# Moving tiles within 128 bytes: start addresses of tails, convolution, gate and keys in a two-layer decoder trunk

## The chip, the cores and the metric

One of the cores of a Trainium2 chip runs the whole program. The metric is device time in microseconds of that core. The times shown are three runs of the kernel before; the profile is of one further execution of the same program.

## What is computed

The reference is a trunk of two layers, on one sequence of 512 tokens with 1024 channels in float32. Each layer is a half-step SwiGLU feed-forward block (FFN), a token mixer and another half-step FFN. The mixer of the first layer is a short gated convolution, that of the second is native sparse attention (NSA). Each sub-layer normalises its input and modulates it with a shift, a scale and a gate computed from a conditioning vector:

```python
h = adaln(x, norm_g[i, 0], shift[:, 0], scl[:, 0])
x = x + HALF * gate[:, 0, None, :] * swiglu(h, ffn_w_in[i, 0], ffn_w_out[i, 0])
h = adaln(x, norm_g[i, 1], shift[:, 1], scl[:, 1])
y = short_conv_mixer(h, ...) if i % N_MIXERS == 0 else nsa_mixer(h, ...)
x = x + gate[:, 1, None, :] * y
h = adaln(x, norm_g[i, 2], shift[:, 2], scl[:, 2])
x = x + HALF * gate[:, 2, None, :] * swiglu(h, ffn_w_in[i, 1], ffn_w_out[i, 1])
```

`swiglu` is `(silu(g) * u) @ w_out` with `g, u = h @ w_in` and 2816 hidden channels. There are four FFNs, one convolution and one NSA.

## The kernel before, in words

The kernel keeps x as eight tiles of 128 channels by 512 tokens. Weights are streamed from HBM as 128x1024 tiles. Every product is made of three matmuls (`mm3`, lines 179 to 181): operand and weight are split into a high and a low part of type float32r (`split`, line 170 on ScalarE, line 171 on VectorE), and high x high, high x low and low x high are summed. In a matmul the weight tile is the held operand (it is loaded into the array by an LDWEIGHTS), and the activation is the streamed one, with 512 columns (all tokens) or 256 (one half of them). The names in the profile are, for example, `gu<-hhi,whi`: output, streamed, held.

The stages follow each other in program order: FFN 0 (`ffn_first`), convolution (`conv`), FFN 1 and 2 (`ffn`), NSA (`nsa`), FFN 3 (`ffn`).

- `ffn_first` and `conv` begin with a head start (`hs`) on a few weight tiles while the normalised input h is still being made, and go on with 512-column products: `gu` in `ffn_first`, `cv` in `conv`. In the FFNs `Hidden` holds the activated hidden channels as tiles `ahi` and `alo` in the pool `fa`; the output products `y` stream them.
- `ffn` makes its head start with 256 columns, then a gate (one weight tile `wh`, `wl`, on the two halves of h), one more pair, and then `seven_products` for the other 18 hidden blocks j = 4 to 21. These multiply by blocks of 2x2 with seven products instead of eight; they stream h and the tiles `th`, `tl` made by `Norm.quarters` and hold `whi`, `wlo`, `qah`, `qal`, `qbh` and `qbl`. After blocks of hidden channels come output products `y`, three rounds of 144 matmuls in each `ffn`.
- Each FFN and the mixers end with a tail (`ty`): the last output products, done for the first 256 tokens and then for the others, so that the norm of the next stage (sums of squares on line 264, reciprocal root on lines 210 to 218, spread over the partitions by the matmul on line 272, then `Norm.piece` on lines 321 to 324) can begin on the first half. In `ffn` the tail has four weight tiles; the last two are split into the buffers of `th`, `tl` (tags t..2 and t..0).
- In `conv` the tail's three weight tiles are in a pool of their own, `tw`. In NSA, keys `K` are streamed against held queries `Q` (line 1068, `s<-k,q`).

The order on each engine is that of the program, but for parts marked as of high priority. A tile waits for the last readers of the buffer that it takes over. All DMAs of weights are issued by SyncE, but for an accumulating one by GpSimd on line 516.

Where a tile begins in a partition is settled by the allocator. Pools are stacked from both ends of SBUF, those with `side="right"` from the top down. `shift(p, n)` (a tile of n bytes that nothing reads or writes) moves what is stacked after it. As the listing stands before the change, the starts within 128 bytes are: 0 for `fa` (`ahi`, `alo`), for the weight pools `wp` and `ada`, for `sw` (`qah`, `qal`, `qbh`, `qbl`), for h in `ffn_first` and `conv`, for z in `conv`, and for K and Q; 64 for h in `ffn` and `nsa`, for `th` and `tl` (and so for the gate's `wh`, `wl`, which use the same buffers) and for `tw`.

Of the kernel before, what the change touches and what calls it, by code (L numbers as in the profile page):

```python
# [13 lines left out]
F32 = mybir.dt.float32  # L14
F32R = mybir.dt.float32r
# [7 lines left out]
P = 128  # L23
D = 1024
T = 512
HT = T // 2
KD = D // P
# [26 lines left out]
def decoder_kernel(ctx, tc, xT, cT, ng, adaw, adab, ffi, ffo, cwi, cw, cwo,  # L54
# [3 lines left out]
    def pool(es, name, bufs, **kw):  # L58
        kw.setdefault("reuse_waits", "tile")
        return es.enter_context(tc.tile_pool(name=name, bufs=bufs, **kw))  # L60


    def shift(p, n):
        p.tile([P, n // 4], F32, name="shift")
# [118 lines left out]
    def weights(src, nk, ncol, own=None, held=3, raws=None, to=None, added=False):  # L183
        def part(name, dt, bufs, from_):
            return (from_ or wp).tile([P, nk * ncol], dt, name=name, tag=name, padded_shape=[P, KD * P], bufs=bufs)

        hi, lo = to or (part("whi", F32R, held, own), part("wlo", F32R, held, own))
        raws = raws or own
        raw = part("wraw", F32, 3 if raws in (None, wp) else 2, raws)
        nc.sync.dma_start(raw.rearrange("p (a n) -> p a n", a=src.shape[1]), src)  # L190
        if added:
            split_added(raw, src, hi, lo)
        else:
            split(raw, hi, lo)
        return [t.rearrange("p (k n) -> p k n", n=ncol) for t in (hi, lo)]
# [28 lines left out]
    class Halves:  # L224
        def __init__(self, *t):
            self.t = t
# [5 lines left out]
    class Norm:  # L232
# [91 lines left out]
            nc.vector.scalar_tensor_tensor(self.lo[d][:, a:b], xr, sh, hi, op0=ALU.add, op1=ALU.subtract)  # L324

        def quarters(self, tt):
            self.th, self.tl = [[tt.tile([P, KD // 2, HT], F32R, name=f"t{e}{j}", tag=f"t{e}{j}") for j in range(4)] for e in "hl"]
            for d in range(KD):
                nc.scalar.activation(self.full[:, d], self.full[:, d], AF.Identity, bias=mod(self.s, 1, d))
            n = KD // 2  # L330
            b11, b12 = self.full[:, 0:n, 0:HT], self.full[:, 0:n, HT:T]
            b21, b22 = self.full[:, n:KD, 0:HT], self.full[:, n:KD, HT:T]
            t = b11, b22, b12, b21
            nc.vector.tensor_tensor(t[0], b11, b12, ALU.subtract)
            nc.vector.tensor_tensor(t[2], b22, b12, ALU.subtract)
            nc.vector.scalar_tensor_tensor(t[1], t[0], -1.0, b22, op0=ALU.mult, op1=ALU.subtract)
            nc.vector.scalar_tensor_tensor(t[3], t[1], -1.0, b21, op0=ALU.mult, op1=ALU.subtract)
            for j in (2, 0, 3, 1):
                split(t[j], self.th[j], self.tl[j])
            self.blocks = [(lambda i, j=j: (self.th[j][:, i, :], self.tl[j][:, i, :])) for j in range(4)]  # L340
# [62 lines left out]

    class Hidden:
        def __init__(self, es, bufs):
            self.fa = pool(es, "fa", bufs, side="right")
            self.hi, self.lo = [], []

# [83 lines left out]
    def ffn(s, f, nrm, nxt, w0, ahead):  # L492
        with ExitStack() as es:
            hp = pool(es, "hp", 1)
            hid = Hidden(es, 12)
            keep = hid.keep
            nj = 2
# [58 lines left out]
                keep(e[:, 0:2].rearrange("p a b -> p (a b)"))  # L556

            js = [(j, c) for j in range(nj) for c in range(2)]
            shift(pool(es, "gap", 1, side="right"), 448)
            tt = pool(es, "tt", 1, side="right")  # L560
            swa = pool(es, "swa", 1, side="right")
            with ExitStack() as tf_es:
                nrm.alloc_seven(hp, pool(tf_es, "tf", 1))
                h = nrm.hi, nrm.lo
                with ExitStack() as hw_es:
                    hw = pool(hw_es, "hw", 1)
                    shift(hw, 64)
                    w = w0 + [weights(ffi[f, j, c], KD, P, hw, 1, wp) for j, c in js[len(w0):]]

                    gate = weights(ffi[f, nj, 0], KD, P, to=[tt.tile([P, D], F32R, name="w" + e, tag=f"t{e}1") for e in "hl"])  # L570
                    os = head_start(nrm, h, [(lambda k, w=w_: (w, 0, k)) for w_ in w])
                os += pair(f, nj, h, gate=gate)
                nrm.quarters(tt)
            sw_es = es.enter_context(ExitStack())

            own, quarter = (partial(swa.tile, [P, 2, KD * P // 2], F32, name="qa", bufs=2),
                            [partial(hp.tile, [P, 2, KD * P // 2], F32, name="qa", tag=t) for t in ("hhi1", "hlo1")])
            sums = chain((own, own, own), cycle((*quarter, own, own)))
            sw = pool(sw_es, "sw", 1)
            shift(sw, 64)  # L580
            for j in range(nj + 1):
                hid.activate(os[2 * j], os[2 * j + 1])
# [2 lines left out]
            for p, (j0, j1) in enumerate(FOUR):  # L585
# [3 lines left out]
                a = (hid.hi[j0:j1], hid.lo[j0:j1])  # L589
                if p < len(FOUR) - 1:  # L590
                    outputs(range(KD), lambda d: ffn_out(f, d, 1, j0, j1), a, n,
                            lambda d, o: nc.vector.scalar_tensor_tensor(x[d], o, mod(s, 2, d), x[d], op0=ALU.mult, op1=ALU.add))  # L592
            sw_es.close()


            ws = []
            for i, d in enumerate(range(0, KD, 2)):
                if i < 2:
                    ws.append(ffn_out(f, d, 2, j0, j1))
                else:  # L600
                    t = (2, 0)[i - 2]
                    to = [tt.tile([P, KD // 2, HT], F32R, name=f"t{e}{t}").rearrange("p a b -> p (a b)") for e in "hl"]
                    raw = swa.tile([P, 2, KD * P // 2], F32, name="qa", bufs=2).rearrange("p a b -> p (a b)")
                    nc.sync.dma_start(raw.rearrange("p (a n) -> p a n", a=2),
                                      ffo[f, d:d + 2, :, j0 * P:j1 * P].rearrange("d p c -> p d c"))
                    split(raw, *to)
                    ws.append([t.rearrange("p (k n) -> p k n", n=P) for t in to])
# [22 lines left out]
    def conv(s, nrm, nxt, extra, w0, ahead, own):  # L630
        with ExitStack() as es:
            h_es = es.enter_context(ExitStack())
            hp = pool(h_es, "hp", 1)
            shift(hp, 256)
            ca = pool(es, "cva", 2, side="right")
            h = nrm.alloc(hp)
            ks = [(k, k) for k in range(KD)]
            zh, zl = [], []
            fill = spread(extra, 2 * KD - 3)
            for d in range(KD):  # L640
                if d == 0:
                    w = w0 + [weights(cwi[3], KD, P, own)]
                    *os, nx = head_start(nrm, h, [(lambda k, w=w_: (w, 0, k)) for w_ in w])
                else:
                    os = [nx] if d == 1 else []
                    for c in range(len(os), 3):
                        w = weights(cwi[3 * d + c], KD, P, own if (d + c) % 2 else None)
                        o = psum("cv")
                        project(o, w, 0, h, ks, True, True)
                        os.append(o)  # L650
                cg, v, b = os
                cs = tmp("cs")
                nc.scalar.activation(cs, cg, AF.Copy)
                u = ca.tile([P, T + 2], F32, name="u")
                nc.vector.memset(u[:, 0:2], 0.0)
                nc.vector.tensor_mul(u[:, 2:], cs, v)
                y = tmp("yc")
                nc.vector.tensor_scalar(y, u[:, 2:], cws[:, 2 * KD + d:2 * KD + d + 1], None, op0=ALU.mult)
                for i in (1, 0):
                    nc.vector.scalar_tensor_tensor(y, u[:, i:i + T], cws[:, i * KD + d:i * KD + d + 1], y,  # L660
                                                   op0=ALU.mult, op1=ALU.add)
                z = tmp("z")
                nc.vector.tensor_mul(z, y, b)
                hi = ca.tile([P, T], F32R, name="zhi", bufs=KD)
                lo = ca.tile([P, T], F32R, name="zlo", bufs=KD)
                split(z, hi, lo)
                zh.append(hi)
                zl.append(lo)
                fill()
            z = (zh, zl)  # L670
            h_es.close()
            tw = pool(es, "tw", 1, side="right")
            for d in range(KD - 3):
                w = weights(cwo[d], KD, P)
                o = psum("y")
                project(o, w, 0, z, ks, True, True)
                residual(s, d, o, nxt)
                fill()
            assert not extra
            return tail(s, nxt, [(d, weights(cwo[d], KD, P, tw), 0, ks) for d in range(KD - 3, KD)], z, ahead)  # L680
# [26 lines left out]
    def nsa(s, nrm, nxt, w0, ahead):  # L707
        with ExitStack() as es:
            na = pool(es, "na", 1, side="right")
# [99 lines left out]
            def run(jobs):  # L809
                for j in jobs:  # L810
                    j()

            K = [[na.tile([P, T], F32R, name=f"k{b}{e}") for e in range(2)] for b in range(2)]
            Q = [na.tile([P, T], F32R, name=f"q{q}") for q in range(NG)]
            keys, heads = turners(qn, kn, K, Q)
            with ExitStack() as hw_es:
# [529 lines left out]
```

## Time and profile before

| what | value |
|---|---|
| time, median of 3 runs | 1957.31 us (1955.87 to 1958.6) |
| profiled execution | 1955.17 us, span 1953.4 us |
| TensorE busy, matmuls | 1902.4 us (97%), 12600 |
| VectorE / ScalarE / GpSimd busy | 1456.4 (75%) / 883.6 (45%) / 211.6 us (11%) |
| granted TensorE clock | 1.0 over the span |
| HBM read | 308.15 MB, 159 GB/s over the span |

The page's first part gives the busy time of each engine; a busy TensorE need not be at its peak, because matmuls overlap in the pipeline. A group's row gives its line, engine and operation, the names out<-in, the shape, the count, the busy time, the mean of one in ns and the idle time before it. A matmul's duration includes its way through the pipeline; how fast matmuls follow each other is read from their start times in the timeline.

### The profile page before, as it was taken

Reading aid. Unit: us, or ns where it says so; the run is one execution under the profiler, and the core shown is the slowest. Engines: PE = TensorE matmul, PEld = TensorE weight load, DVE = VectorE, ACT = ScalarE, POOL = GpSimd, SP = SyncE. Lnnn points to the kernel's source line nnn. Section 1 sums busy time; section 2 is a strip of 40 time slices with the busy share of each in tenths; the row PEclk is TensorE's granted clock in tenths of the full one; section 3 lists DMA queues with packets and bytes.
Section 4 is the critical chain, followed back from the end, with each engine's and each line's share of the span. In section 5 each row is a group of like instructions: output and inputs, shape, how many; then the busy total and the mean of one; then the engine's idle time right before and its main releaser. Section 6 shows DMA issues by size and latency. Waiting matters only on the chain.

```text
span 1953.4 us, 32342 instructions
## 1 busy us (share of the span) xinstructions
PE 1902.4 (97%) x12600; PEld 1725.7 (88%) x12600; DVE 1456.4 (75%) x2557; ACT 883.6 (45%) x1425; POOL 211.6 (11%) x302
## 2 busy tenths in 40 slices
PE   5999999999999999999999999999999899999999
PEld 3878888898899898999989899999888789898989
DVE  7878888674467596878859687885787878686965
ACT  3322222242236353444635343465888966353532
POOL 0000000100010000000000000001445630000000
PEclk9999999999999999999999999999999999999999
DMA  8888899522235564634556453235423523765621
GB/s 311 303 321 325 313 320 328 205 98 97 67 120 162 155 173 132 160 103 126 156 156 173 134 158 103 78 130 139 112 60 68 125 74 113 188 167 143 173 82 65
DMA packets 113671, 313.42 MB, mean 160 GB/s; under 512 B 13996, under 2 KB 14268, under 8 KB 113517
## 3 DMA queue, kind: packets, MB, share of 16 engines
q1 hardware_dynamic: 96300, 274.02, 41.2%
q0 software_dynamic: 17216, 37.33, 11.1%
q8 instruction: 99, 1.62, 0.3%
q14 instruction: 56, 0.45, 0.1%
HBM read 308.15 MB, written 3.15 MB: 159 GB/s over the span
## 4 chain that ended last, share of the span: by engine, by line
PE 85%; DVE 7%; ACT 4%; issue 2%; DMA 1%; SPq 0%; POOL 0%; DVEq 0%; ACTq 0%
PE gu L181 13%; PE gu L180 13%; PE gu L179 13%; PE y L179 7%; PE y L180 7%; PE y L181 7%; PE hs L180 2%; PE hs L179 2%; PE hs L181 2%; PE cv L179 2%; PE cv L181 2%; PE cv L180 2%; PE ty L180 2%; PE ty L179 1%; PE ty L181 1%
## 5 line engine op out<-in xcount | busy, mean ns | idle before, releaser
L170 ACT ACTIVATE whi<-wraw 128x1024 fp32r<-128x1024 f32 (+2 forms) x274 | 270.7, 996 | 507.3 <-PE y L180 218.3
L171 DVE TENSOR_TENSOR wlo<-wraw,whi 128x1024 fp32r<-128x1024 f32 (+2 forms) x274 | 312.9, 1147 | 57.9 <-ACT whi L170 55.6
L179 PE MATMUL gu<-hhi,whi 128*128 128x256 f32 (+1 forms) x880 | 277.6, 315 | 0.0
L181 PE MATMUL gu<-hhi,wlo 128*128 128x256 f32 (+1 forms) x880 | 277.5, 315 | 0.0
L180 PE MATMUL gu<-hlo,whi 128*128 128x256 f32 (+1 forms) x880 | 277.5, 315 | 0.0
L179 PE MATMUL y<-ahi,whi 128*128 128x512 f32 x587 | 228.6, 389 | 0.0
L180 PE MATMUL y<-alo,whi 128*128 128x512 f32 x587 | 228.5, 389 | 0.0
L181 PE MATMUL y<-ahi,wlo 128*128 128x512 f32 x587 | 228.3, 389 | 0.0
L125 DVE CUSTOM_DVE_ANT_0 adaraw<-adaraw,cond 128x1024 f32<-128x1024 f32 x144 | 174.8, 1223 | 40.4 <-DMA adaraw<-in_adaw 38.2
L180 PEld LDWEIGHTS gu<-hlo,whi 128*128 128x128 f32 x880 | 165.1, 188 | 12.2
L179 PEld LDWEIGHTS gu<-hhi,whi 128*128 128x128 f32 x880 | 165.2, 188 | 12.1
L181 PEld LDWEIGHTS gu<-hhi,wlo 128*128 128x128 f32 x880 | 165.2, 188 | 12.0
L516 POOL DMA_DIRECT2D qa<-in_ffi x54 | 65.0, 1205 | 793.2 <-DMA qa<-in_ffi 275.9
L179 PEld LDWEIGHTS y<-ahi,whi 128*128 128x128 f32 x587 | 110.2, 188 | 23.3 <-issue 0.8
L181 PEld LDWEIGHTS y<-ahi,wlo 128*128 128x128 f32 x587 | 110.2, 188 | 23.1
L180 PEld LDWEIGHTS y<-alo,whi 128*128 128x128 f32 x587 | 110.2, 188 | 22.5
L592 DVE SCALAR_TENSOR_TENSOR x<-y,mods,x 128x512 f32<-128x512 f32 x72 | 53.4, 750 | 92.5 <-PE y L181 92.4
L179 PE MATMUL gu<-th,qbh 128*128 128x256 f32 x432 | 119.5, 277 | 1.0 <-ACT qbh L170 1.0
L181 PE MATMUL gu<-th,qbl 128*128 128x256 f32 x432 | 119.6, 277 | 0.6 <-DVE qbl L171 0.5
L180 PE MATMUL gu<-tl,qbh 128*128 128x256 f32 x432 | 119.3, 276 | 0.0
L179 PE MATMUL gu<-th,qah 128*128 128x256 f32 x432 | 119.2, 276 | 0.0
L180 PE MATMUL gu<-tl,qah 128*128 128x256 f32 x432 | 119.2, 276 | 0.0
(312 smaller groups left out, 5094.8 us busy)
## 6 DMA issues: line engine op xcount, KB each, us to landing
adaraw<-in_adaw SPq DMA_DIRECT2D x144, 512.0 KB, 6.0
wraw<-in_ffi SPq DMA_DIRECT2D x122, 512.0 KB, 4.0
qa<-in_ffi SPq DMA_DIRECT2D x108, 256.0 KB, 3.7
qa<-in_ffi POOLq DMA_DIRECT2D x54, 512.0 KB, 6.3
wraw<-in_ffo SPq DMA_DIRECT2D x72, 384.0 KB, 3.9
a<-in_ffi SPq DMA_DIRECT2D x54, 256.0 KB, 4.5
wraw<-in_cwi SPq DMA_DIRECT2D x24, 512.0 KB, 3.3
wraw<-in_nwi SPq DMA_DIRECT2D x20, 512.0 KB, 3.8
```

The costliest lines, as they stand in the source:

```text
L125: nc.vector.tensor_tensor_reduce(out=raw, in0=raw, in1=cond, scale=1.0, scalar=0.0, op0=ALU.mult, op1=ALU.add, accum_out=m)
L170: nc.scalar.activation(hi, src, AF.Copy)
L171: nc.vector.tensor_tensor(lo, src, hi, ALU.subtract)
L179: nc.tensor.matmul(o, sh, mh, start=first, stop=False)
L180: nc.tensor.matmul(o, sh, ml, start=False, stop=False)
L181: nc.tensor.matmul(o, sl, mh, start=False, stop=last)
L516: nc.gpsimd.dma_start(qa, bass.AP(tensor=a21.tensor, offset=a21.offset, ap=[a21.ap[0], [0, 2], a21.ap[1]]), accum_op=ALU.add)
L592: lambda d, o: nc.vector.scalar_tensor_tensor(x[d], o, mod(s, 2, d), x[d], op0=ALU.mult, op1=ALU.add))
```

## The change

No instruction is added or taken away. Seven places move tiles:

- `Hidden` stacks 64 bytes before `fa`, so `ahi` and `alo` begin 64 bytes within 128 (in all four FFNs); in `ffn` the later shift of 448 becomes 384, so `th` and `tl` stay at 64.
- The buffers of tags th1 and tl1 are 128 bytes longer; the gate uses them from byte 64 on, so `wh` and `wl` begin at 0.
- The last two weight tiles of the tail in `ffn` go to the buffers of `qah` and `qal` in the pool `sw` (0) instead of `th2`, `tl2`, `th0`, `tl0` (64); `sw` is closed with the other pools.
- `conv`: h moves by 64 (256 becomes 320), and 64 bytes are stacked before the pool of z, so z begins at 64 and `tw`, stacked after it, at 0.
- `nsa`: 64 bytes before K and 64 after, so K begins at 64 and Q, stacked after it, stays at 0.

```diff
         def quarters(self, tt):
-            self.th, self.tl = [[tt.tile([P, KD // 2, HT], F32R, name=f"t{e}{j}", tag=f"t{e}{j}") for j in range(4)] for e in "hl"]
+            self.th, self.tl = [[tt.tile([P, T * KD // 4 + 32 * (j == 1)], F32R, name=f"t{e}{j}", tag=f"t{e}{j}")[:, 0:T * KD // 4]
+                                 .rearrange("p (a b) -> p a b", b=HT) for j in range(4)] for e in "hl"]
...
         def __init__(self, es, bufs):
+            shift(pool(es, "fs", 1, side="right"), 64)
             self.fa = pool(es, "fa", bufs, side="right")
...
-            shift(pool(es, "gap", 1, side="right"), 448)
+            shift(pool(es, "gap", 1, side="right"), 384)
...
-                    gate = weights(ffi[f, nj, 0], KD, P, to=[tt.tile([P, D], F32R, name="w" + e, tag=f"t{e}1") for e in "hl"])
+                    gate = weights(ffi[f, nj, 0], KD, P, to=[tt.tile([P, D + 32], F32R, name="w" + e, tag=f"t{e}1")[:, 16:16 + D] for e in "hl"])
...
-            sw_es = es.enter_context(ExitStack())
-
...
-            sw = pool(sw_es, "sw", 1)
+            sw = pool(es, "sw", 1)
...
-            sw_es.close()
...
-                    t = (2, 0)[i - 2]
-                    to = [tt.tile([P, KD // 2, HT], F32R, name=f"t{e}{t}").rearrange("p a b -> p (a b)") for e in "hl"]
+                    to = [sw.tile([P, 2, KD * P // 2], F32R, name=f"qa{e}", bufs=2).rearrange("p a b -> p (a b)") for e in "hl"]
...
-            shift(hp, 256)
+            shift(hp, 320)
+            shift(pool(es, "cs", 1, side="right"), 64)
             ca = pool(es, "cva", 2, side="right")
...
+            na.tile([P, 16], F32, name="shift")
             K = [[na.tile([P, T], F32R, name=f"k{b}{e}") for e in range(2)] for b in range(2)]
+            na.tile([P, 16], F32, name="shift2")
             Q = [na.tile([P, T], F32R, name=f"q{q}") for q in range(NG)]
```

## The prediction

> **What bounds the kernel now.** I read the page's totals and its chain of waits first.
>
> ```profile
> span 1953.4 us, 32342 instructions
> PE 1902.4 (97%) x12600; PEld 1725.7 (88%) x12600; DVE 1456.4 (75%) x2557; ACT 883.6 (45%) x1425; POOL 211.6 (11%) x302
> PE 85%; DVE 7%; ACT 4%; issue 2%; DMA 1%; SPq 0%; POOL 0%; DVEq 0%; ACTq 0%
> ```
>
> TensorE sets the end: 85% of the chain, and no other engine has more than 7%. A nanosecond per matmul is worth 12.6 us, so the question is at what step the matmuls follow each other, and what depends on the addresses there. I write 64/0 for "streamed operand begins 64, held operand 0 bytes within 128"; these starts are sums of tile sizes in the listing, not readings of the profile. The next view is the groups of matmuls by form (busy time, then mean ns of one).
>
> ```profile
> L179 PE MATMUL y<-ahi,whi 128*128 128x512 f32 x587 | 228.6, 389 | 0.0
> L179 PE MATMUL gu<-th,qah 128*128 128x256 f32 x432 | 119.2, 276 | 0.0
> L179 PE MATMUL cv<-hhi,whi 128*128 128x512 f32 x160 | 62.3, 389 | 0.0
> L180 PE MATMUL y<-zlo,whi 128*128 128x512 f32 x40 | 15.6, 389 | 0.0
> L180 PE MATMUL ty<-alo,whi 128*128 128x256 f32 x138 | 39.3, 285 | 0.0
> L180 PE MATMUL ty<-alo,th 128*128 128x256 f32 x96 | 27.0, 281 | 0.0
> L180 PE MATMUL ty<-zlo,whi 128*128 128x256 f32 x48 | 13.5, 281 | 0.0
> L180 PE MATMUL gu<-hlo,wh 128*128 128x256 f32 x48 | 13.6, 283 | 0.0
> ```
>
> The form is the same 128x256 in five of these rows, but one takes 276 ns (64/0: the seven products), one 283 (64/64: the gate), one 285 with its waits (0/0: the tails) and two 281 (0/64: tails with th or z). A duration holds the pipeline too; the step comes from starts in the timeline (column 1 is the start).
>
> ```profile
> 610.73 0.28 PE L180 MATMUL gu<-hlo,whi 128*128 128x256 f32 x1
> ...
> 620.59 0.28 PE L180 MATMUL gu<-hlo,whi 128*128 128x256 f32 x1
> ...
> 1937.85 0.28 PE L179 MATMUL ty<-ahi,whi 128*128 128x256 f32 x1
> ...
> 1943.49 0.28 PE L181 MATMUL ty<-ahi,wlo 128*128 128x256 f32 x1
> 1943.61 0.28 PE L179 MATMUL ty<-ahi,th 128*128 128x256 f32 x1
> ...
> 1949.15 0.28 PE L181 MATMUL ty<-ahi,tl 128*128 128x256 f32 x1
> ```
>
> At 64/0, 87 steps take 9.86 us, 0.1133 each. At 0/0, 47 steps take 5.64 us, 0.1200. At 0/64, 47 steps take 5.54 us, 0.1179. So duration less about 163 ns is the step, and a 256-column matmul could lose 6.7 ns (from 0/0 or 64/64) or 4.5 ns (from 0/64). A 512-column one at 0/0 already goes at 389 - 163 = 226, twice 113: it has nothing to win.
>
> **The change part by part.** No instruction is added or removed; tiles move.
>
> *256-column matmuls brought to 64/0.* Rows have three lines each (L179, L180, L181), so counts are three times a row's. Tails on whi/wlo: 3 x 138 = 414, from 0/0, 414 x 6.7 ns = 2.8 us. Tails on the FFN's last weights: 3 x 96 = 288, from 0/64, 1.3 us. Tail of the convolution: 3 x 48 = 144, from 0/64, 0.65 us. Gate: 144, from 64/64, 0.96 us. Head start of the convolution, whose h moves from 0 to 64:
>
> ```profile
> L179 PE MATMUL hs<-hhi,whi 128*128 128x256 f32 x34 | 9.6, 283 | 0.0
> L179 PE MATMUL hs<-hhi,whi 128*128 128x256 f32 x36 | 9.9, 276 | 0.0
> ```
>
> The first row is that head start (409 to 421 us), the second the same code in an FFN (929 to 941 us), already at 64/0. It has 4 jobs x 8 x 2 halves x 3 = 192, 1.3 us. Together 7.0 us.
>
> *What of it reaches the end.* The last tail (1926 to 1949 us) has nothing behind it but the output: 0.64 + 0.43 = 1.1 us in full. The gate lies ahead of a wait in the same stage, so I looked at what that wait hangs on (chain of waits, start, length, what):
>
> ```profile
> 620.52 0.13 PE gu L181
> 620.65 0.23 SPq L513
> 620.97 0.39 SPq L513
> 621.42 6.11 DMA a<-in_ffi
> 627.55 0.64 ACT qbh L170
> ```
>
> The transfer that ACT waits for is issued when a TensorE group behind the gate ends, so it moves with TensorE and the gate's gain passes. It is otherwise in the tails before a norm. There the second half runs beside VectorE's reciprocal root, residuals and weight splits (windows; busy and count of PE, PEld, DVE, ACT):
>
> ```profile
> 390.70:397.30 6.60, 6.60 (x53) 6.42 (x53) 6.04 (x21) 2.73 (x4) 0.00 (x0) 1.00 0.25 82
> 907.00:917.20 10.20, 10.20 (x84) 9.95 (x84) 9.06 (x28) 5.17 (x10) 0.00 (x0) 1.00 0.30 104
> ...
> 917.25 0.28 PE L181 MATMUL ty<-ahi,tl 128*128 128x256 f32 x1
> 918.29 0.75 PE L179 MATMUL hs<-hhi,whi 128*128 128x256 f32 x4 [0.76 <-ACT hhi L323]
> ```
>
> VectorE is busy 92% and 89% there, and TensorE then stands until ACT has hhi: a faster second half only lengthens that wait. I count the second half of those three tails as covered: FFN 2 x (48 x 6.7 + 48 x 4.5) = 1.1 us, first tail 63 x 6.7 = 0.4 us. If the cover is thinner than it looks, up to 1.5 us more comes through. Sum: 7.0 - 1.5 = 5.5 us.
>
> *The tail's last weights in sw instead of tt.* Their first buffer is then free after the product with s1 of j = 20, not of the last j; the second is freed by the same product of j = 21 as before. Nothing is later, so 0.
>
> *Keys at 64.* The profile has no 64/0 row of this form among the scores; 64 matmuls of 128x256 stand between 0 and 64 x 6.7 = 0.4 us. Their stage is full of waits on VectorE, so I take 0.
>
> *512-column matmuls that also go from 0/0 to 64/0.* These come along because hid, h and z move: y on ahi/alo 3 x 587 = 1761, cv 480, y on z 120, in all 2361. The only 64/0 run of 512 columns in the trace is the NSA gates' projection:
>
> ```profile
> L179 PE MATMUL gl<-hhi,whi x8: 390/394/394, 1330.8 to 1335.6; 128*128 128x512 f32 x8
> L180 PE MATMUL gl<-hlo,whi x8: 388/388/398, 1331.0 to 1335.8; 128*128 128x512 f32 x8
> L181 PE MATMUL gl<-hhi,wlo x8: 392/392/394, 1331.3 to 1336.1; 128*128 128x512 f32 x8
> ```
>
> Medians 394, 388, 392 make 391.3 on average, 2.3 ns above the 389 of 0/0, and it stays so over all 24. At that price: 2361 x 2.3 ns = 5.4 us, as much as is won. But the step is not a function of the residues alone. The same line with the same operands has two steady values:
>
> ```profile
> L179 PE MATMUL hs<-hhi,whi 128*128 128x256 f32 x14 | 3.9, 279 | 0.0
> L180 PE MATMUL nat<-wlo,hhi 128*128 128x256 f32 x27 | 7.6, 281 | 0.0
> L180 PE MATMUL nat<-wlo,hhi 128*128 128x256 f32 x31 | 8.6, 276 | 0.0
> ```
>
> hs at 64/0 ran at 279 to 280 from 1261.8 to 1266.5 us and at 276 in the FFN row above; nat at 0/64 ran at 281 (1285 to 1294 us) and at 276 (1350 to 1361 us). A run keeps the step it entered with until something disturbs it. gl was entered from such a slower stretch; the y blocks will be entered from gu at 276. Bounds 0 and +5.4 us; I take 0, because the state ahead of y is the fast one in all seven-product rows. A gain below 226 per step has no row and is left out.
>
> Against the profiled execution (1955.17 us: span 1953.4 plus 1.8) this gives 1949.7; the median shown, 1957.31, lies 2.1 above that execution, so 1957.3 - 5.5 = **1951.8 us**.
>
> **The rivals.**
>
> *The wide matmuls take the slower step.* For it: gl, 24 of 24. Against it: gl's entry. With all 2361, -5.5 + 5.4, 1957.2 us; with one group alone (first FFN's y 465: +1.1; conv 600: +1.4; other y 1296: +3.0) 1952.9 to 1954.8.
>
> *The tails stay in the slow state.* The sums of squares interrupt each tail, and each re-entry may land at 281. Then 0/0 and 64/64 win 750 x 2.2 ns = 1.6 us and the rest nothing; with the cover about 1.3: 1956.0 us. Against it: of the FFN head starts that such interruptions cut up, most run at 276.
>
> *Slower: the y blocks hand a slow step on.* Now y at 0/0 always hands over to gu at 276. If y at 64/0 hands it 281, the seven products behind it (16 per FFN x 84 x 3 FFNs = 4032) each lose 4.5 ns: 18.1 us, with y's own 3.0: 1951.8 + 21.1 = 1972.9 us. The place is the first gu after each y block; it decides from 5.5 + 3.9 = 9.4 us of loss, about 2100 of those matmuls. For it: the hs row at 279, which is 64/0. Against it: the other 64/0 rows.
>
> *The addresses do nothing.* The steps would belong to the stages, not to the starts, and nothing changes: 1957.3 us. Against it: one code line, one form, 283 and 276 in two head starts. The Trainium skill ("TensorE: Matmul & The Clock Gate", "Step-by-step: what each phase is for") says that streamed operand and weights have independent read ports, so that "Loading the next tile's weights doesn't steal SBUF read bandwidth from the running matmul", and ("SBUF — State Buffer", "Who interferes with whom") that PE never waits on anyone. By that rule this rival is right; the trace disagrees, with 283 against 276.
>
> **How the numbers follow.** Forecast 0.49; wide matmuls slower 0.25; tails slow 0.10; slow step handed on 0.10; nothing 0.06. About 0.2%, 3.9 us, is what a measurement here tells from no change. Faster than 1953.4: nearly all of the forecast and a little of the second case, 0.48. Slower than 1961.2: the fourth and a little more, 0.11. The rest, 0.41, is the same. The likeliest case alone reaches from 1949.9 (7.0 + 0.4, no cover) to 1953.5 (one tail or one group slow). The range for 8 in 10 takes in the wide matmuls' 1957.2 and no change with its scatter: 1949.9 to 1958.0.
>
> **What would show it.** In the groups by form: ty at 276 to 278 instead of 281 to 285, gu<-hlo,wh 276, the conv head start 276: these show the gain. y and cv at 389 show the wide ones unharmed, 391 the second case. gu<-th at 276 clears the fourth, 280 confirms it. The wait before hs at 918 longer by about 0.5 us shows the cover. The prediction is wrong if the 256-column rows keep their durations, or if they fall and the span does not.

## The result

The change made the kernel slower: 1978.32 us (median of 4 runs, 1975.47 to 1979.94) against 1957.95 us before (4 runs, 1955.87 to 1958.84). The ratio is 1.0103, 95% interval 1.0088 to 1.0118, which is +20.4 us. The prediction was 1951.8 us.

The page of the kernel after: totals and the chain of waits by engine.

```profile
span 1976.3 us, 32341 instructions
PE 1922.0 (97%) x12600; PEld 1731.4 (88%) x12600; DVE 1457.1 (74%) x2557; ACT 885.6 (45%) x1425; POOL 211.7 (11%) x302
PE 85%; DVE 7%; ACT 4%; DMA 2%; issue 2%; SPq 0%; POOL 0%; DVEq 0%; ACTq 0%
```

TensorE still sets the end with the same 12600 matmuls, and its busy time rose by 19.6 us, most of the 22.9 us by which the span grew. The busy times of the other engines changed by 2 us or less. So the matmuls became slower, and the groups by form (busy time, then mean ns of one) say which:

```profile
L179 PE MATMUL y<-ahi,whi 128*128 128x512 f32 x587 | 232.7, 396 | 0.0
L179 PE MATMUL gu<-th,qbh 128*128 128x256 f32 x432 | 120.6, 279 | 1.7 <-ACT qbh L170 1.7
L180 PE MATMUL cv<-hlo,whi 128*128 128x512 f32 x160 | 62.7, 392 | 0.0
L180 PE MATMUL ty<-alo,whi 128*128 128x256 f32 x138 | 38.6, 279 | 0.0
L180 PE MATMUL ty<-alo,qah 128*128 128x256 f32 x96 | 26.6, 277 | 0.0
L180 PE MATMUL y<-zlo,whi 128*128 128x512 f32 x40 | 15.8, 395 | 0.0
L180 PE MATMUL ty<-zlo,whi 128*128 128x256 f32 x48 | 13.5, 280 | 0.0
L180 PE MATMUL gu<-hlo,wh 128*128 128x256 f32 x48 | 13.2, 276 | 0.0
```

The small rows behaved as hoped: the tails fell from 285 and 281 ns to 279 and 277, the gate from 283 to 276. The wide rows paid for it: y on hidden went from 389 to 396, y on z from 389 to 395, cv from 389 to 392. And gu on th, whose operands mostly stayed where they were, rose from 276 or 277 to 277 with qah and 279 with qbh. The timeline of one output block and what follows it (column 1 is the start) shows the steps:

```profile
649.58 0.39 PE L179 MATMUL y<-ahi,whi 128*128 128x512 f32 x1
...
683.17 0.28 PE L179 MATMUL gu<-hhi,whi 128*128 128x256 f32 x1
...
695.90 0.28 PE L179 MATMUL gu<-th,qah 128*128 128x256 f32 x1
...
699.86 0.28 PE L181 MATMUL gu<-th,qbl 128*128 128x256 f32 x1
```

144 matmuls of y take 33.59 us, 233.3 ns each. The next 108 matmuls take 12.73 us, 117.9 each; the 35 behind them 3.96 us, 113.1 each. The same place before:

```profile
642.46 0.39 PE L179 MATMUL y<-ahi,whi 128*128 128x512 f32 x1
...
675.12 0.28 PE L179 MATMUL gu<-hhi,whi 128*128 128x256 f32 x1
...
677.95 0.28 PE L179 MATMUL gu<-th,qah 128*128 128x256 f32 x1
...
679.99 0.28 PE L179 MATMUL gu<-th,qah 128*128 128x256 f32 x1
```

There y takes 32.66 us, 226.8 each, and only 24 matmuls behind it go at 117.9; from 677.95 on it is 113. So y hands a slow step on to gu in both kernels, 24 matmuls long before and 108 long after: 84 x 4.5 ns = 0.38 us for each of nine such blocks.

The last view is the windows (busy time and count of PE, PEld, DVE, ACT, POOL, then the granted clock). After:

```profile
134.50:138.20 3.70, 3.70 (x9) 2.55 (x9) 3.67 (x6) 1.51 (x2) 0.00 (x0) 0.54 0.96 303
1278.00:1281.60 3.60, 3.60 (x19) 3.60 (x19) 2.83 (x12) 1.23 (x3) 0.00 (x0) 0.53 0.46 146
```

Twice the clock was granted at half for about 3.4 us, which costs at most 1.7 us each time; the profile before has it whole in the same stretch (1.00 from 134.5 to 138.2 us). The first of the two does not come from the change: it stands at the end of the eight products `pt<-oh,rbn`, and 9 of the 12 profiles of the experiments below have it there too, for 3.4 or 6.8 us, whatever they move. The times scatter with this clock (of 27 runs of before, 8 at a mean clock of 1.0 have a median of 1955.92 us, 11 at 0.999 one of 1957.29, 7 at 0.998 one of 1958.90), and as the profiled execution of before has it at 1.0, the two spans lie 22.9 us apart and the medians 20.4.

**Where the time went**, span against span (22.9 us), read from the lag, that is by how much a matmul starts later than the same matmul of before:

| where the lag grows, and what is there | us |
|---|---|
| ahead of the first y, where no matmul reads a moved tile | +1.3 |
| y on hidden, 465 x 6.7 ns in the first FFN and 1296 x 6.4 ns | +11.4 |
| hand-over from y to gu, 9 x 84 x 4.5 ns | +3.4 |
| th1 and tl1 (padding of the gate's buffers, below), behind these stretches | +2.1 |
| cv, 480 x 2.2 ns; y on z, 120 x 6.6 ns | +1.8 |
| clock at half near 134 us | +1.3 |
| from the gate to the first y, three FFNs (gate, th1, wait for qbh) | +0.2 |
| tails and norms behind FFN 1 and 2 (faster tails, longer waits before hs, clock at half near 1278 us) | +2.5 |
| first tail and head start of the convolution (lag 5.9 before it, 5.2 behind) | -0.7 |
| last tail (22.7 to 21.9 us from its first to its last matmul) | -0.8 |
| the rest | +0.4 |
| sum | +22.9 |

The first term and the clock near 134 us, 2.6 us together, are scatter between executions: the kernels below with unmoved weights start their first gu between 64.7 and 66.3 us (before 64.9, after 66.2). Without the two, the spans lie as far apart as the medians.

### The profile page after: what moved, and what is told of

It is laid out like the page before. It is cut to its first block, busy times and chain, and to the rows that moved or that the text cites. A ratio compares the mean times of both kernels' runs of the same rounds, so it can differ in the third digit from the quotient of the medians.

```text
span 1976.3 us, 32341 instructions
## 1 busy us (share of the span) xinstructions
PE 1922.0 (97%) x12600; PEld 1731.4 (88%) x12600; DVE 1457.1 (74%) x2557; ACT 885.6 (45%) x1425; POOL 211.7 (11%) x302
## 4 chain that ended last, share of the span: by engine, by line
PE 85%; DVE 7%; ACT 4%; DMA 2%; issue 2%; SPq 0%; POOL 0%; DVEq 0%; ACTq 0%
PE gu L181 13%; PE gu L179 13%; PE gu L180 13%; PE y L179 8%; PE y L181 8%; PE y L180 8%; PE hs L179 2%; PE hs L181 2%; PE hs L180 2%; PE cv L181 2%; PE cv L180 2%; PE cv L179 2%; PE ty L180 1%; PE ty L179 1%; PE ty L181 1%
## 5 line engine op out<-in xcount | busy, mean ns | idle before, releaser
L179 PE MATMUL gu<-hhi,whi 128*128 128x256 f32 (+1 forms) x880 | 277.8, 316 | 0.0
L180 PE MATMUL gu<-hlo,whi 128*128 128x256 f32 (+1 forms) x880 | 277.8, 316 | 0.0
L179 PE MATMUL y<-ahi,whi 128*128 128x512 f32 x587 | 232.7, 396 | 0.0
L181 PE MATMUL y<-ahi,wlo 128*128 128x512 f32 x587 | 232.4, 396 | 0.0
L180 PE MATMUL y<-alo,whi 128*128 128x512 f32 x587 | 232.4, 396 | 0.0
L179 PEld LDWEIGHTS gu<-hhi,whi 128*128 128x128 f32 x880 | 165.2, 188 | 12.3
L180 PEld LDWEIGHTS gu<-hlo,whi 128*128 128x128 f32 x880 | 165.1, 188 | 12.2
L179 PEld LDWEIGHTS y<-ahi,whi 128*128 128x128 f32 x587 | 110.6, 188 | 27.2 <-issue 0.9
L180 PEld LDWEIGHTS y<-alo,whi 128*128 128x128 f32 x587 | 110.6, 188 | 26.4
L179 PE MATMUL gu<-th,qbh 128*128 128x256 f32 x432 | 120.6, 279 | 1.7 <-ACT qbh L170 1.7
L180 PE MATMUL gu<-tl,qbh 128*128 128x256 f32 x432 | 120.4, 279 | 0.0
L179 PE MATMUL gu<-th,qah 128*128 128x256 f32 x432 | 119.6, 277 | 0.0
L180 PE MATMUL gu<-tl,qah 128*128 128x256 f32 x432 | 119.6, 277 | 0.0
```

What stands on the lines that cost most here:

```text
L179: nc.tensor.matmul(o, sh, mh, start=first, stop=False)
L180: nc.tensor.matmul(o, sh, ml, start=False, stop=False)
L181: nc.tensor.matmul(o, sl, mh, start=False, stop=last)
```

## The experiments

Starts are now given within 256 bytes, as sums of tile sizes in the listing; "difference" is the streamed start less the held one, within 256. Before, y, cv and y on z stream from 128 and hold at 128 (difference 0). After, y and y on z stream from 64 (difference 192), cv streams from 192 (difference 64). All of that is "64/0" within 128.

**The parts alone.** First the hidden tiles:

```diff
         def __init__(self, es, bufs):
+            shift(pool(es, "fs", 1, side="right"), 64)
...
-            shift(pool(es, "gap", 1, side="right"), 448)
+            shift(pool(es, "gap", 1, side="right"), 384)
```

> The hidden tiles alone begin 64 instead of 0 bytes within 128; all else is the kernel before. Theory A (the wide matmuls carry the loss): the 1761 y on the hidden tiles last 396 ns instead of 389 in the mean, 1761 x 6.6 ns = +11.6 us, and the products behind each y block in the three later FFNs start at the slow step (about 108 matmuls x 4.5 ns x 9 blocks = +4.4 us); the tails on whi gain 414 x 5.5 ns = -2.3, those on th lose 288 x 2.2 = +0.6; together +14 us, most of the 20 us. Rival B (the loss sits in the other edits, convolution, gate and buffers): y stays near 389 without them and the time moves by less than 3 us.

Measured 1971.85 us against 1958.12: 1.0069 (1.0051 to 1.0087), +13.7 us. Its groups by form:

```profile
L179 PE MATMUL y<-ahi,whi 128*128 128x512 f32 x587 | 232.7, 396 | 0.0
L179 PE MATMUL gu<-th,qah 128*128 128x256 f32 x432 | 119.6, 277 | 0.0
L180 PE MATMUL ty<-alo,whi 128*128 128x256 f32 x138 | 38.8, 281 | 0.0
L179 PE MATMUL y<-zhi,whi 128*128 128x512 f32 x40 | 15.6, 389 | 0.0
```

This part carries two thirds of the loss: y at 396, while y on z, not moved here, stays at 389. The tails win less than in the full change (281 instead of 279), because here the products on whi stay at a step of 117.8, and those on the last weights, at difference 128, take 118.3 to 118.7.

All but the hidden tiles, as against the full change:

```diff
-            shift(pool(es, "fs", 1, side="right"), 64)
...
-            shift(pool(es, "gap", 1, side="right"), 384)
+            shift(pool(es, "gap", 1, side="right"), 448)
```

> The changed kernel with the hidden tiles back at 0. Theory A: y on the hidden tiles is 389 again, the products behind y are at 276 from the start; left are cv +1.1, y on z +0.8, the products on th1/tl1 at 281 (648 x 4.2 ns = +2.7), tails on the last weights now 0/0 +0.6, gate and head start -0.9; together +4 us over before (1962). Rival B: nearly all of the +20 us stays.

Measured 1964.44 us: 1.003 (1.0017 to 1.0043), +6.3. That is 2.3 us more than expected; the move of the last weights to `sw` costs as much further below, by the order of the work, which this expectation left out. With the first experiment it makes 20.0 of 20.4. The convolution alone:

```diff
-            shift(hp, 256)
+            shift(hp, 320)
+            shift(pool(es, "cs", 1, side="right"), 64)
```

> Only the convolution's edits (h at 64, z at 64, its tail's weights at 0). Theory A: cv 391 (480 x 2.2 ns = +1.1 us), y on z 396 (+0.8), head start 281 instead of 283 (-0.4), tail hardly changed: +1.5 us. If the step depended on the start within 128 alone, cv would be at 396 like y and cost 480 x 6.6 = +3.2 us, together +3.6 us.

Measured 1959.72 us: 1.0007 (0.9998 to 1.0016), +1.6. The interval holds no change, so the rows decide. Its groups by form hold both steps at once: cv at difference 64, y on z at 192.

```profile
L180 PE MATMUL cv<-hlo,whi 128*128 128x512 f32 x160 | 62.7, 392 | 0.0
L180 PE MATMUL y<-zlo,whi 128*128 128x512 f32 x40 | 15.8, 395 | 0.0
```

The gate's edit alone (buffers of th1 and tl1 128 bytes longer, gate from byte 64):

```diff
-            ... tt.tile([P, KD // 2, HT], F32R, name=f"t{e}{j}", tag=f"t{e}{j}") ...
+            ... tt.tile([P, T * KD // 4 + 32 * (j == 1)], F32R, name=f"t{e}{j}", tag=f"t{e}{j}")[:, 0:T * KD // 4] ...
-            ... tt.tile([P, D], F32R, name="w" + e, tag=f"t{e}1") ...
+            ... tt.tile([P, D + 32], F32R, name="w" + e, tag=f"t{e}1")[:, 16:16 + D] ...
```

> Only the gate's edit: 128 bytes more in the buffers of th1/tl1, gate at 0. It moves th1 by 256 and tl1 by 128 bytes. Theory A: the gate falls from 283 to 276 (-0.96 us at most, part of it lost to the wait behind it), the 648 products on th1/tl1 rise from 276 to 280 or 281 (+2.7 us): +2 us in all. Rival: the th1/tl1 step in the changed kernel was handed on by y and is 276 here; then -0.3 to -0.9 us.

Measured 1961.32 us: 1.0018 (1.0008 to 1.0029), +3.2. Its timeline, a product with th3 and the one with th1 behind it, 12 matmuls each:

```profile
731.39 0.28 PE L179 MATMUL gu<-th,qbh 128*128 128x256 f32 x1
...
732.75 0.28 PE L179 MATMUL gu<-th,qbh 128*128 128x256 f32 x1
...
734.16 0.28 PE L179 MATMUL gu<-hhi,qbh 128*128 128x256 f32 x1
```

The first takes 1.36 us, 113.3 each, the second 1.41, 117.5. Padding each of the two buffers by 128 bytes moves the tiles stacked behind them by different amounts: tl1 moves by 128 bytes and th1 by 256. The streamed starts of that product then alternate between 64 and 192. With 256 bytes of padding both stay at 192:

```diff
-            ... T * KD // 4 + 32 * (j == 1) ...    [P, D + 32]
+            ... T * KD // 4 + 64 * (j == 1) ...    [P, D + 64]
```

> Only the gate's edit, but with 256 instead of 128 bytes added to the buffers of th1 and tl1, so that all streamed tiles keep their start within 256 and the gate still begins at 0. Difference theory: gate 276 and the products on th1/tl1 276, -0.3 to -1.0 us. If the longer buffers as such, or a gate at 0, cost the 3.2 us of the 128-byte edit: +2 to +3 us.

```profile
732.51 0.28 PE L179 MATMUL gu<-th,qbh 128*128 128x256 f32 x1
...
733.87 0.28 PE L179 MATMUL gu<-th,qbh 128*128 128x256 f32 x1
...
735.23 0.28 PE L179 MATMUL gu<-hhi,qbh 128*128 128x256 f32 x1
```

Both products take 1.36 us. Measured 1957.27 us against 1957.32: 0.9999 (0.999 to 1.0008). The loss is gone, and the gate's own gain is too small to be seen.

**Which property of the addresses counts for the 512-column matmuls?** The hidden tiles were moved by 128 and by 192 bytes instead of 64. Within 128 those are 0/0 again and 64/0 again; the differences are 128 and 64.

```diff
+            shift(pool(es, "fs", 1, side="right"), 128)    # the other: 192
...
-            shift(pool(es, "gap", 1, side="right"), 448)
+            shift(pool(es, "gap", 1, side="right"), 320)   # the other: 256
```

> The hidden tiles alone moved by 128 bytes: they begin 0 bytes within 128 as in the kernel before, but 128 from the held weights within 256. Difference theory (the step of a 512-column matmul goes by streamed minus held start within 256: 0 gives 226.7 ns, 64 gives 229, 192 gives 233.3): y between, near 231.5 a step (394 as a duration), 1761 x 4.8 ns = +8 us, with 0 to 4.4 us more if the products behind y start slow. Parity theory (only the start within 128 counts): y stays at 389, no change.

> The hidden tiles alone moved by 192 bytes: 64 bytes within 128 as in the first of these experiments, but 64 instead of 192 from the held weights within 256. Difference theory: y at 229 a step (391 to 392), 1761 x 2.3 ns = +4 us; tails on whi -2.5, on th +0.6; 0 to 4.4 for the products behind y: +2 to +6.5 us. Parity theory: y at 396 again and +14 us as there.

By 128 bytes: 1969.54 us, 1.0063 (1.0047 to 1.0078), +12.2. Its timeline:

```profile
740.05 0.39 PE L179 MATMUL y<-ahi,whi 128*128 128x512 f32 x1
...
773.50 0.28 PE L179 MATMUL gu<-hhi,whi 128*128 128x256 f32 x1
```

144 in 33.45 us, 232.3 each (233.3 in the first FFN): the same starts within 128 as before, and slow. By 192 bytes: 1959.83 us, 1.0015 (1.0005 to 1.0024), +2.5, and this timeline:

```profile
680.50 0.28 PE L179 MATMUL gu<-hhi,whi 128*128 128x256 f32 x1
...
692.75 0.28 PE L179 MATMUL gu<-th,qah 128*128 128x256 f32 x1
...
737.62 0.39 PE L179 MATMUL y<-ahi,whi 128*128 128x512 f32 x1
...
770.59 0.28 PE L179 MATMUL gu<-hhi,whi 128*128 128x256 f32 x1
```

y steps at 32.97 / 144 = 229.0 ns, and the 108 gu behind a y block take 12.25 us, 113.4 each, with no hand-over at all, less than before had. The starts within 128 are those of the change in both places. So they decide nothing here, and the slow gu is left behind by y, since gu has the same addresses in all these kernels.

In all runs so far the weights were held at 128, so a rule on the streamed start alone would have fitted as well. The next two kernels move the held weights by 64 bytes (and put h of the first FFN and the convolution back where it was; h in `ffn` and `nsa` moves with the weights); the second also moves the hidden tiles, so that y alone has difference 0.

```diff
+    shift(pool(ctx, "ws", 1), 64)
     wp = pool(ctx, "wp", 4)
...
-            shift(hp, 256)          # first FFN and convolution
+            shift(hp, 192)
...
-            shift(sw, 64)           # and those of hw and nw
...
+            shift(pool(es, "fs", 1, side="right"), 192)    # second kernel only, gap 256
```

> Only the held weights move: the pools wp and ada begin 64 bytes later, the activations that 512-column matmuls stream stay where they were before (streamed 128 within 256 bytes, held 192 instead of 128). Theory of the difference (what counts is streamed minus held start within 256 bytes, here 192): y, cv, y on z and the 512-column gu of the first FFN all step at 233.3 ns, their rows at 396 instead of 389; 1761 + 480 + 120 + 912 = 3273 matmuls by 6.6 ns = +21.6 us, up to +3.4 for the hand-over to gu, and +4.3 for the 648 gu on qbh that come to 0/0, +1.3 for head starts at 0/0, less about 1.5 for tails: about +29 us, 1986. Theory of the streamed start alone: these rows stay at 389, and the total is +4, 1961. gl (streamed 0, held 192) is 391 by the difference, 395 or more by the streamed start.

> As the run with moved weights, and the hidden tiles moved by the same 64 bytes (streamed 192, held 192 within 256): the difference is 0 again for y on hidden alone; cv, y on z and the 512-column gu keep 192. Theory of the difference: y 389, cv and gu 396; the total is +3.2 +6.0 +0.8 for these, +4.3 for gu on qbh, +1.3 head starts, +0.6 for tails at 64/64: about +16 us, 1973. Theory of the streamed start alone: y 392 (as with hidden tiles moved by 192 under unmoved weights), cv and gu 389; total about +9.5, 1967.

Measured 1990.37 us, 1.0165 (1.0151 to 1.0179), +32.9, and 1982.93 us, 1.0124 (1.0109 to 1.014), +25.5, against 1957.46. Groups by form of the kernel with moved weights (its lines are numbered one higher, L180 for L179):

```profile
L180 PE MATMUL y<-ahi,whi 128*128 128x512 f32 x587 | 232.2, 396 | 0.0
L180 PE MATMUL gu<-th,qah 128*128 128x256 f32 x432 | 121.2, 280 | 0.0
L180 PE MATMUL gu<-hhi,whi 128*128 128x512 f32 x304 | 120.2, 396 | 0.0
L180 PE MATMUL cv<-hhi,whi 128*128 128x512 f32 x160 | 63.3, 395 | 0.0
L181 PE MATMUL ty<-alo,th 128*128 128x256 f32 x96 | 26.5, 276 | 0.0
```

The activations of y, gu and cv lie where before had them at 389; with the weights moved, all three go at 396. With the hidden tiles moved as well, y alone returns (timeline: 144 in 32.67 us, 226.9 each), while cv in that kernel stays at 396:

```profile
747.49 0.40 PE L180 MATMUL y<-ahi,whi 128*128 128x512 f32 x1
...
780.16 0.28 PE L180 MATMUL gu<-hhi,whi 128*128 128x256 f32 x1
```

The theory of the difference holds for these rows, and the streamed start alone falls. gl, whose h moved with the weights and so kept difference 64, stays at medians of 392, 394 and 388 ns. But one kernel below, which moves nothing that gl reads (the last four hidden blocks at 64), has gl at

```profile
L179 PE MATMUL gl<-hhi,whi x8: 396/397/398, 1335.2 to 1340.1; 128*128 128x512 f32 x8
```

and its two other lines alike: a step of 233.3 ns instead of 229 at the same starts. The kernel with all but the hidden tiles has it as well. At difference 64 the starts do not settle the step alone; what else does is open.

Both totals were above the expectation, the second by about 9 us. The main reason is the row of gu on th, alike in both: 280 instead of 276, though its operands did not move. It now alternates with products of h and qbh that came to 0/0, and 2592 matmuls by 3.6 ns are 9.3 us. A slow step is carried into neighbours that would be fast by themselves. Against that, the first expectation had up to 3.4 us for the hand-over behind y, which did not come: the slow stretch there is 27 or 28 matmuls long instead of 108.

**The rest: keys and last weights.** The two parts left, keys at 64 and the tail's last two weight tiles in `sw`:

```diff
-            sw_es = es.enter_context(ExitStack())
-            sw = pool(sw_es, "sw", 1)
+            sw = pool(es, "sw", 1)
...
-            sw_es.close()
...
-                    to = [tt.tile([P, KD // 2, HT], F32R, name=f"t{e}{t}")...
+                    to = [sw.tile([P, 2, KD * P // 2], F32R, name=f"qa{e}", bufs=2)...
...
+            na.tile([P, 16], F32, name="shift")     # before K, and once more behind it
```

> The two parts not yet run alone: keys at 64, and the tail's last weights in sw. The single parts so far add to 18.5 us of the 20.4; if these two carry the rest it is +1.9 us. By the steps they change little: the last tail weights come to streamed 128 and held 0, a step of 118.5 instead of 117.8, 288 x 0.7 = +0.2; the keys lie among waits: -0.4 to 0. Expected 0 (-0.4 to +0.5), with ty on qah at 282.

Measured 1959.76 us: 1.0009 (1.0 to 1.0018), +2.3, an interval that just reaches no change. The four single parts (13.7, 1.6, 3.2, 2.3) now add to 20.8 of 20.4. The steps do not explain these 2.3 us (ty on qah 281 to 285); the order of the work does. VectorE's timeline of this kernel:

```profile
920.21 1.22 DVE L171 TENSOR_TENSOR wl<-wraw,wh 128x1024 fp32r<-128x1024 f32 x1
921.37 0.48 DVE L348 SCALAR_TENSOR_TENSOR x<-ty,mods,x 128x256 f32<-128x256 f32 x1
921.77 0.47 DVE L321 SCALAR_TENSOR_TENSOR hfull<-x,mods,pr 128x256 f32<-128x256 f32 x1
```

and of before:

```profile
917.21 0.48 DVE L321 SCALAR_TENSOR_TENSOR hfull<-x,mods,pr 128x256 f32<-128x256 f32 x1
...
924.55 1.22 DVE L171 TENSOR_TENSOR wl<-wraw,wh 128x1024 fp32r<-128x1024 f32 x1
```

With `sw` held to the end of the tail, the order on VectorE has the split of the gate's wl, 1.22 us, ahead of the first hfull; before it came 7 us after it. hhi waits for hfull, and TensorE for hhi. The waits of TensorE in this kernel around that place (before: 0.8):

```profile
PE hs L179 <- ACT hhi L323: 1.5, 1, 1.5
```

At the norm ahead of NSA a wait of 1.0 us for hlo (VectorE, L324) comes on top of the 0.8 us for hhi. From the tail ahead of the first of these norms to the first y behind it the lag grows from 3.75 to 5.00 us, and across the second to 6.24: 2.5 us, about the whole cost. The keys are no part of it: from the first to the last score the stage takes 215.35 us here and 215.38 before.

So the change is not one of addresses alone. The order is the program's, so the full change has it too (wl at 927.87 us, hfull at 929.42).

**Is there a version that wins?** In `ffn`, only the last four hidden blocks are streamed in the tail, so only they were put 64 bytes further (streamed 192, held 128 or 0), and the last weights went to `sw` as in the change; y there has none of these tiles:

```diff
...
+                b = 16 if j >= self.late else 0
+                hi, lo = (self.fa.tile([P, T + 64], F32R, name=n, tag="b", bufs=8)[:, b:b + T] for n in ("ahi", "alo"))
...
-            hid = Hidden(es, 12)
+            hid = Hidden(es, 12, FOUR[-1][0])
...
-            shift(pool(es, "gap", 1, side="right"), 448)
+            shift(pool(es, "gap", 1, side="right"), 192)
```

> The kernel before with only those hidden tiles moved to 64 that the tails of the three later FFNs stream and no y does (the last four of each), and those tails' last weights in the buffers of qah/qal at 0; all y stay 0/0. If the tails win at 64/0 and y was the whole loss: 576 tail matmuls, 288 x 6.7 + 288 x 4.5 ns = -3.2 us, of which the halves beside the norm may be covered: -2 us (-1 to -3.2). If the tails fall into the slow step after each interruption by the norm: 281 and -0.6 us or nothing.

Measured 1957.21 us against 1957.32: 1.0001 (0.9992 to 1.0009). y kept 389, and the tails got their step (ty on whi 280, on qah 277), the last tail 21.65 us from first to last matmul instead of 22.71. But the windows at the two norms behind the other tails read:

```profile
920.20:923.80 3.60, 3.60 (x20) 3.60 (x19) 3.60 (x17) 1.43 (x3) 0.00 (x0) 0.53 0.02 6
...
1261.50:1268.40 6.90, 6.74 (x31) 6.74 (x32) 5.85 (x24) 2.50 (x5) 0.00 (x0) 0.51 0.22 76
```

Half the clock for about 3.4 and 6.8 us, behind waits before hs of 1.6 us and 0.8 + 1.0 us (before: 0.8 and 0.8). The last kernel keeps this one's tiles and leaves the last weights in `tt`, as against the one above:

```diff
+            sw_es = es.enter_context(ExitStack())
-            sw = pool(es, "sw", 1)
+            sw = pool(sw_es, "sw", 1)
...
+            sw_es.close()
...
-                    to = [sw.tile([P, 2, KD * P // 2], F32R, name=f"qa{e}", bufs=2)...
+                    to = [tt.tile([P, KD // 2, HT], F32R, name=f"t{e}{t}")...
```

> As the run with the last four hidden blocks at 64, but the tail's last two weight tiles stay in the buffers of th and tl as before. Theory A: the longer wait before hs (1.6 us at 918 where before had 0.8) and the halved clock behind it came from the placement of those weights in sw, which puts VectorE's split of the gate's wl (1.22 us) ahead of hfull; then here that split stands behind hfull as before, the wait is 0.8 to 1.3 us, the clock is whole between 915 and 930 us, and the total is the tails' gain: 288 x 6.7 = 1.9 less 288 x 2.2 = 0.6 for the weights left at 64/64, about half of it covered: -0.7 us (-1.3 to +0.3). Theory B: the tails' own gain lengthens the wait; then the wait is 1.6 us again, the clock halves there, and the total is 0.

Measured 1957.04 us against 1958.32: 0.9993 (0.9984 to 1.0002). The wait in the same two places is alike:

```profile
PE hs L179 <- ACT hhi L323: 0.8, 1, 0.8
```

The clock is 1.00 over 915 to 930 and 1255 to 1275 us. The tails here are fast on whi only (113.3; 120 on th), but in the kernel with moved weights they run at 113.3 throughout, and its wait is 0.8 us too. So the longer waits and the halved clock there came from the placement in `sw`, not from a faster tail. By the starts, the tails bring 0.2 us at each of the two norms and 0.4 us at the end, 0.8 us in all. The measured -1.3 us fits that, but its interval holds no change; no version of this study is shown to beat the kernel before.

## Why the prediction was wrong

**The step that failed** is "Bounds 0 and +5.4 us; I take 0, because the state ahead of y is the fast one in all seven-product rows". Both the value and the upper bound were wrong: the 2361 wide matmuls cost 13.2 us. The reason for the value fell in one row: y enters from gu at 113 and steps at 233.3 all the same. The bound fell because the starts were described within 128 bytes. gl, from which 2.3 ns was read, has difference 64, and cv, which got the same difference, cost just that (228.9 instead of 226.7). y and y on z got 192 and cost 6.5. The three groups were put under one price, and 1761 of the 2361 matmuls had another. The needed starts, modulo 256, were in the listing.

**"Now y at 0/0 always hands over to gu at 276" was a misreading.** 24 matmuls behind each y block ran at 117.9 before, as the starts from 675.12 to 677.95 us show; the mean of 276 over 432 hid them.

**The rival of the slow step handed on** named the right place and mechanism and was nearest in time (1972.9), but that nearness is luck. It let the slow step last for all 4032 matmuls, 18.1 us, and gave y 3.0 us; the slow step lasts 84 more per block, 3.4 us, and y itself paid 11.4. It had 0.10.

**The rival of the slower wide matmuls** (1957.2) was right about what happens and too small by the same mis-sized price. **The rival that the addresses do nothing** is refuted: with the weights alone moved, one row goes from 389 to 396. The Trainium skill's rule that PE never waits on anyone ("SBUF — State Buffer", "Who interferes with whom") is about one engine waiting for another; it says nothing of starts, and no run here tests it.

**The padding of th1 and tl1 has no term in the sum.** The longer buffers were counted as the gate's gain alone; by themselves they cost 3.2 us, and by the two products above that is because they put th1 and tl1 at different starts within 256.

**The gains came only in part.** Without the gate the sum had 4.5 us that reach the end; the lag shows about 2.0. The last tail gave 0.8 of 1.1 us, and 1.06 with the last four hidden blocks at 64. The first tail and the convolution's head start gave 0.7 of 1.7: the head start came to 64/0 and ran at 117.8, not 113.3, which the rival of the slow tails described. The convolution's tail kept 280 (0 of 0.65). The first halves of the tails of FFN 1 and 2 gave 0.5 of 1.1. In the full change the tails of the three later FFNs run at 117.8 for their first 54 matmuls and at 113.3 from there. They did not take that step over: the six matmuls right ahead of them go at 113.3, and with the hidden tiles alone moved all 36 do. With the hidden tiles at 192 instead of 64 within 256 they run at 113.3 from the first.

**The gate** went to 276, but the claim that its gain passes was not borne out: the wait behind it on ACT's qbh grew from 0.8 to 1.2 us in FFN 1, with a transfer of 6.45 us instead of 6.11. In the eight kernels without the gate's edit and with unmoved weights this wait is 0.5 to 1.2 us, in the four with the edit 1.0 to 1.9. Part of the gain seems to go into it; how much, waits that scatter so widely do not say.

**"Nothing is later, so 0" for the weights in sw** failed in the other direction: something came earlier, wl's split, and stood in front of hfull. With the keys, which change nothing, it cost 2.3 us (0 to 3.5 by the interval).

**The cover** (1.5 us of the tails' gain swallowed by the norm) was right in size and wrong in place. In the kernel with moved weights the tails run at 113.3 throughout, with no placement in `sw`. There the first half of FFN 1's tail takes 10.88 us instead of 11.41, and hs begins 24.70 us after the tail's start instead of 25.19: the first half's gain arrives, the second half's does not. It goes into two waits for VectorE inside the tail, which before has not:

```profile
926.82 0.61 PE L265 MATMUL pr<-ones,nacc 128*128 128x1 f32 x4 [0.21 <-DVE nacc L248]
...
936.63 0.70 PE L273 MATMUL pr<-dg,ones 128*128 128x256 f32 x2 [0.37 <-DVE dg L272]
938.45 0.73 PE L180 MATMUL hs<-hhi,whi 128*128 128x256 f32 x4 [0.76 <-ACT hhi L324]
```

The wait before hs stays at 0.8 us, so the sign that the prediction named for the cover does not show.

## What to carry to other kernels

Before moving a tile, list every matmul that streams or holds it, with both starts to 256 bytes and not to a coarser unit, and price each group by a measured row of the same column count and the same difference; the group with the most matmuls decides, here 1761 against some 1,200 that gain. Look at starts in the timeline right behind each change of group, since a row's mean hides a stretch of 24 slow matmuls. And an edit that keeps a buffer longer is not an edit of addresses: compare the order on every engine as well.

## What the runs showed of the hardware

**A 512-column float32r matmul's step went with the difference of the two starts within 256 bytes**: 226.7 to 226.9 ns at 0, 228.9 to 229.6 at 64, 232.3 to 233.3 at 128, 233.3 to 233.4 at 192. The steps at 0, 64 and 192 were seen with weights held at 128 and at 192. At 64 the rule has an exception: gl ran at 233.3 in two kernels. What makes it so inside the chip is not shown.

**For 256 columns equal starts are the slowest, and the step has a memory.** Difference 0 gave 120.0 ns, 128 gave 118.3 to 118.8, 64 and 192 gave 113.3 or 117.8. The last two values can belong to the same starts: in the kernel with moved weights the tails on th, whose operands did not move, ran at 113.3 instead of 117.8. Behind y at 232.3 or 233.3 with the weights at 128, gu kept the slow step for 108 matmuls (once for 24); behind y at 227 for 24; behind y at 229 for none. With moved weights it kept it for 27 or 28, behind y at 233.3 as behind y at 226.9. It was also carried into gu on th between products at 0/0. What starts and ends such a stretch is open.

**Half the clock came behind short pauses, and also without one.** Four kernels have the last weights in `sw`. At the norm behind FFN 1 they wait 1.5 to 1.6 us, and the clock then halves for 3.4 us in two and stays whole in two, the kernel of the change among them. At the norm ahead of NSA they wait 0.8 and 1.0 us, and it halves for 3.4 or 6.8 us in three. In the ten others, which wait 0.8 us, it stays whole at both places. Near 134 us it halves in 10 of the 14 profiles at the end of the eight products `pt<-oh,rbn` (33 by 512), with no pause ahead of it. The Trainium skill ("TensorE: Matmul & The Clock Gate", "What's actually happening") describes a clock gate that passes half the pulses after an idle window of about 3.4 us and judges in free-running windows of that length. The lengths of one and two such windows agree with the rows here, and a window that runs freely fits that runs of one kernel differ in it; but no pause here was as long as 3.4 us, so by these traces a shorter pause, or none, can be enough.
